# Mask additions of the attention loop tied behind the latest sums of products

## Chip, cores and metric

The kernel runs on one core of one Trainium2 chip. The metric is the device time of one execution in microseconds (us). A core has a matmul engine (TensorE, PE in the profile, with its weight loads as PEld), a vector engine (VectorE, DVE), an activation engine (ScalarE, ACT), a general engine (GpSimd, POOL) and an engine that here only orders transfers (SyncE, SP). Each runs its own queue of instructions in order; semaphores join them.

## The reference, cut to what matters

The program is one inference step of a two-layer trunk over 512 prompt tokens and 8 x 16 sample tokens: a gMLP layer, then a layer of forgetting attention (FoX) with 16 heads of 128. The change touches the attention alone:

```python
def fox_attend_prompt(q, k, v, logf):      # 512 queries, in blocks of 128
    cT = jnp.cumsum(logf, axis=1).transpose(0, 2, 1)
    ...
        s = jnp.einsum('bqhd,bkhd->bhqk', qi, k).astype(jnp.float32) * scale
        s = s + ci[..., :, None] - cT[:, :, None, :]
        s = jnp.where(key_pos[None, :] <= qpos[:, None], s, -jnp.inf)
        p = jax.nn.softmax(s, axis=-1).astype(v.dtype)
        return jnp.einsum('bhqk,bkhd->bqhd', p, v)

def fox_attend_sample(q, k_new, v_new, logf_new, k_cache, v_cache, logf_cache):
    # 16 new queries of each sample against 256 cached keys and 16 new ones
    ...
    mask = jnp.arange(P + T)[None, :] <= (P + jnp.arange(T))[:, None]
    s = jnp.where(mask, s, -jnp.inf)
```

The term of the query's own row falls out of the softmax, so the kernel subtracts only a row of cumulated forget logarithms over the keys ("the decay row") from the scores, with 1e30 added where the causal mask forbids a key.

## The kernel before, in words

**Stages.** Up to about 570 us the first layer runs. The attention loop follows, to about 1140 us, and then the second layer's output projection, gate and stores. In the loop, step `p` (0 to 6) does two things at once. TensorE computes four projections, `project_z(p)` for the pair of heads 2p and 2p+1 and `project_v`, `project_k`, `project_q` for the next pair. Between their matmuls stand the *pieces* of the attention of heads 2p and 2p+1. The last pair's attention (p = 7) runs beside `project_z(7)` and the output projection.

**Projections.** Each of the four is written with seven block products instead of eight (`seven_products`). Each product is 12 matmuls (helper `mm3`, lines 271 to 273) into one of four banks (`UZ`), and DVE adds it to the partial sums: lines 573, 575, 578, and line 562 in `total`, four times in a projection (behind its fourth, fifth, sixth and seventh product). That frees the bank. `total` also notes its instruction as the latest one on DVE:

```python
        def total(i, j, a, b):
            behind["dve"] = nc.vector.tensor_tensor(out=into(i, j), in0=a, in1=b, op=ALU.add)
            done(i, j, into(i, j))
```

`project_z` follows each of its totals with a tanh on ACT (line 957) and a product on DVE (line 958). The weights come by transfers from GpSimd's queue, are combined on GpSimd (line 210), and are split into a high and a low part by ACT (lines 288, 291) and DVE (lines 289, 292).

**Prompt pieces.** For each head and each block i of 128 queries, `scores(i)` prepares the masked decay row of the diagonal block (line 993, into one of two small tiles that take turns: `w1s`, shown as R, and `blk`, shown as CST), multiplies the scores on PE, and takes the row maximum while subtracting the decay row: line 1003 for the blocks left of the diagonal, line 1006 for the diagonal block with line 993's tile. ACT exponentiates (line 1010), DVE inverts and scales (lines 1014, 1015), PE transposes (line 1021) and multiplies with the values (line 1028). The decay row of a head is one transfer from `c_sc`, broadcast to 128 partitions (tiles `sff` and CST).

**Sample pieces.** For each pair of heads and each group of four samples (`bg` 0 and 1), `scores` adds the 16-column causal mask to the last columns of `Wc` (line 1074), multiplies on PE (line 1077), takes the row maximum with `Wc` (line 1080), exponentiates on ACT (line 1083), and lets ACT order the next 128x272 mask rows from `cs_sc` into the same `Wc` (`load_mask`). `Wc` exists once. Lines 1089, 1097, 1105, 1112 and 1118 are the rest of this softmax, its transposes and its products. The cached keys come in by 128 KB transfers on SyncE's queue (`load_k`, four for each block, into one tile) and are turned by DVE in `turn_k` (line 1054, four transposes).

**Order.** `interleave` runs a projection and starts each piece when the sum of the planned matmul times passes the piece's time. In a loop step the four projections end at 12.35, 24.7, 37.0 and 49.4 of that time; the two sample scores have the times 5 and 26, the prompt scores 4, 8.8, 13.6, 18.4 for the first head and 23.2, 28, 32.8, 37.6 for the second. That fixes the order in which instructions are traced. The order in each engine's queue is not the traced one: a planner with its own estimates of durations fills the queues (`schedule_with_timeline_sim=True`), and puts an instruction where its inputs are ready by its estimate. A block under `queued("dve")` gives the planner one more rule: each DVE instruction traced in it stands in DVE's queue behind the instruction noted as `behind["dve"]`. It is an order in one queue, with no semaphore. `turn_k` has it already:

```python
        with queued("dve"):
            for bl in range(4):
                nc.vector.transpose(out=kt[:, hh, bl, :PAST], in_=kraw[:, bl])
```

Of the kernel before, what the change touches and what calls it, by code (L numbers as in the profile page):

```python
# [20 lines left out]
ALU = mybir.AluOpType  # L21
# [10 lines left out]
TS = 16  # L32
PAST = 256
# [7 lines left out]
C_ID, C_BLK, C_CM, C_SEL, C_TRI, C_T16, C_M16, C_N = 0, 128, 256, 384, 640, 1152, 1168, 1184  # L41
# [16 lines left out]
def hybrid_trunk(tc, x_prompt, x_sample, ck, cv, clf, p_prompt, p_sample, norm_pre, norm_post,  # L58
                 g_win, ln_g, ln_b, w_s, b_s, g_wout, f_win, b_f, f_wout, w_proj, w_gate, consts,
                 y_p, y_s, st_v, fk_p, fv_p, fl_p, fk_s, fv_s, fl_s):  # L60
    nc = tc.nc
# [12 lines left out]
    CST = sbuf.tile([P, C_N], F32, name="CST")  # L74
# [15 lines left out]
    def r1(o, n, p=P):  # L90
        return R1[:p, o:o + n]
# [6 lines left out]
    def ring(name, lst):  # L98
        i = counters.get(name, 0)
        counters[name] = i + 1  # L100
        return lst[i % len(lst)]

    def bank(lst=(0, 1, 2, 3, 4, 5, 6, 7)):
        return PB[ring(("bank", lst), lst)]
# [21 lines left out]
    @contextmanager  # L126
    def queued(*engines):

        with ExitStack() as stack:
            for e in engines:  # L130
                stack.enter_context(tc.issue_after(behind[e].ins))
            yield
# [145 lines left out]
    causal = CST[:, C_CM:C_CM + P]  # L278
# [184 lines left out]
    for p in range(4):  # L463
# [3 lines left out]
        out = [bank((0, 1, 2, 3, 4, 5, 6, 7)) for _ in range(NT)]  # L467
# [390 lines left out]
    def v_of(p):  # L858
        return r1(o_v + (p % 2) * 1280, 1280).rearrange("p (t n) -> p t n", t=NT)
# [4 lines left out]
    def q_of(h):  # L864
        return both(o_q, h % 2)[:, :512]

    def k_of(h):
        return both(o_k, h % 2)[:, :512]
# [4 lines left out]
    def z_of(h):  # L873
        return both(o_z, h % 2)
# [93 lines left out]
    def w0_of(h):  # L968
        return tri if h % 2 else SF[:, 2048:2560] if h < 14 else r1(o_raw, 512)

    def load_w0(h, queue=None):
        dma(w0_of(h), c_sc[h].partition_broadcast(P), queue)

    def prompt_pieces(h):

        p, hh = h // 2, h % 2
        q, k, v = q_of(h), k_of(h), v_of(p)
        w0 = w0_of(h)
        zs = (NW - 1) * 2048
        qh, ql, kh, kl = (W[:, zs + z * 512:zs + (z + 1) * 512] for z in range(4))  # L980
        O = PB[7]
        prs, pts = {}, {}

        def setup():
            split(kh, kl, k)
            split(qh, ql, q)

        def scores(i):
            n = (i + 1) * P
            d = slice(i * P, n)  # L990
            S = bank(ATT)
            w1 = ring("w1", w1s)
            nc.vector.tensor_tensor(out=w1, in0=w0[:, d], in1=causal, op=ALU.add)
            if i:
                mm3(S[:, :n], (qh[:, d], ql[:, d]), (kh[:, :n], kl[:, :n]), True, True)
            else:
                nc.tensor.matmul(S[:, :n], q[:, d], k[:, :n], start=True, stop=True)
            pr = prs[i] = r1(o_P + ring("P", (0, 1)) * 512, 512)
            m = small()
            init = -3e38  # L1000
            if i:
                m0 = small()
                nc.vector.tensor_tensor_reduce(out=pr[:, :i * P], in0=S[:, :i * P], in1=w0[:, :i * P], scale=1.0, scalar=init,
                                               op0=ALU.subtract, op1=ALU.max, accum_out=m0)
                init = m0
            nc.vector.tensor_tensor_reduce(out=pr[:, d], in0=S[:, d], in1=w1, scale=1.0, scalar=init,
                                           op0=ALU.subtract, op1=ALU.max, accum_out=m)
            nm, sm = small(), small()
            nc.vector.tensor_scalar(out=nm, in0=m, scalar1=-1.0, scalar2=None, op0=ALU.mult)  # L1009
            nc.scalar.activation(out=pr[:, :n], in_=pr[:, :n], func=AF.Exp, bias=nm, accum_out=sm)  # L1010
            if i == 3 and h + 2 < 14:
                load_w0(h + 2, nc.scalar)
            ri = small()
            nc.vector.reciprocal(out=ri, in_=sm)
            nc.vector.tensor_scalar(out=pr[:, :n], in0=pr[:, :n], scalar1=ri, scalar2=None, op0=ALU.mult)  # L1015

        def turn(i):
            n, pr = (i + 1) * P, prs[i]
            tb = bank(ATT)
            for j in range(i + 1):  # L1020
                nc.tensor.transpose(out=tb[:, j * P:(j + 1) * P], in_=pr[:, j * P:(j + 1) * P], identity=ident)
            pt = pts[i] = r1(o_PT + ring("PT", (0, 1)) * 512, 512)
            nc.scalar.activation(out=pt[:, :n], in_=tb[:, :n], func=AF.Copy)

        def values(i):
            d, pt = slice(i * P, (i + 1) * P), pts[i]
            for j in range(i + 1):
                nc.tensor.matmul(O[:, d], v[:, j, hh * P:(hh + 1) * P], pt[:, j * P:(j + 1) * P], start=(j == 0), stop=(j == i))  # L1028
            if i == 3:
                nc.vector.scalar_tensor_tensor(out=y_of(h)[:, :512], in0=O, scalar=0.5, in1=z_of(h)[:, :512], op0=ALU.mult, op1=ALU.mult)  # L1030

        return setup, scores, turn, values
# [27 lines left out]
    Wc = r1(o_Ws, 272)  # L1060
# [4 lines left out]
    def sample_pieces(p, bg):  # L1065

        pr = r1(o_Ps, 400)
        pt = r1(o_PTs, 384)
        os_ = r1(o_Ps, 256)
        kept = {}  # L1070

        def scores():
            S = bank(ATT)
            nc.vector.tensor_tensor(out=Wc[:, PAST:], in0=Wc[:, PAST:], in1=CST[:, C_M16:C_M16 + TS], op=ALU.add)
            for hh in range(2):
                for bl in range(4):
                    nc.tensor.matmul(S[32 * bl:32 * bl + 32, :272], qpads[:, hh, 4 * bg + bl].rearrange("p h q -> p (h q)"),
                                     kt[:, hh, bl], start=(hh == 0), stop=(hh == 1))
            m, nm, sm, ri = small(), small(), small(), small()
            nc.vector.tensor_tensor_reduce(out=pr[:, :272], in0=S[:, :272], in1=Wc, scale=1.0, scalar=-3e38, op0=ALU.subtract,  # L1080
                                           op1=ALU.max, accum_out=m)
            nc.vector.tensor_scalar(out=nm, in0=m, scalar1=-1.0, scalar2=None, op0=ALU.mult)
            nc.scalar.activation(out=pr[:, :272], in_=pr[:, :272], func=AF.Exp, bias=nm, accum_out=sm)
            if 2 * p + bg < 15:
                load_mask(2 * p + bg + 1, nc.scalar)
            nc.vector.reciprocal(out=ri, in_=sm)
            kept["ri"] = ri

            nc.vector.tensor_tensor(
                out=pr[:, 272:].rearrange("p (b k) -> p b k", b=NB),  # L1090
                in0=CST[:, C_SEL + bg * P:C_SEL + (bg + 1) * P].rearrange("p (b k) -> p b k", b=NB),
                in1=pr[:, PAST:272].unsqueeze(1).broadcast_to([P, NB, TS]), op=ALU.mult)

        def turn():
            tb = bank(ATT)
            for j, o_ in enumerate((0, P, 272)):
                nc.tensor.transpose(out=tb[:, j * P:(j + 1) * P], in_=pr[:, o_:o_ + P], identity=ident)
            nc.scalar.activation(out=pt, in_=tb[:, :384], func=AF.Copy)

        def values():  # L1100
            O = bank(ATT)
            nc.tensor.matmul(O[:, :256], pt[:, 256:], v_of(p)[:, 4], start=True, stop=False)
            for t in range(2):
                for bl in range(4):
                    nc.tensor.matmul(O[32 * bl:32 * bl + 32, :256], pt[:, t * P + 32 * bl:t * P + 32 * bl + 32],
                                     vv[:, bl, t], start=False, stop=(t == 1))
            nc.scalar.activation(out=os_, in_=O[:, :256], func=AF.Copy, scale=kept["ri"])

        def gate():
            tb = bank(ATT)  # L1110
            for hh in range(2):
                nc.tensor.transpose(out=tb[:, hh * P:(hh + 1) * P], in_=os_[:, hh * P:(hh + 1) * P], identity=ident)
            for hh in range(2):
                h = 2 * p + hh
                cs = slice(512 + 64 * bg, 512 + 64 * bg + 64)
                y = y_of(h)[:, cs].rearrange("p (b q) -> p b q", b=4)
                o_ = tb[:, hh * P:(hh + 1) * P].rearrange("p (b h q) -> p b h q", b=4, h=2)[:, :, hh, :]
                nc.vector.scalar_tensor_tensor(out=y, in0=o_, scalar=0.5, in1=z_of(h)[:, cs].rearrange("p (b q) -> p b q", b=4),
                                               op0=ALU.mult, op1=ALU.mult)

        return scores, turn, values, gate

    def prompt_times(h, t0, step):
# [107 lines left out]
```

## Time and profile before

| what | before |
|---|---|
| median of 3 runs | 1348.92 us (1347.77 to 1350.22) |
| profiled execution | 1350.09 us, its span 1348.2 us |
| mean granted TensorE clock | 0.990 |
| PE busy in 600 to 1140 us | 499.35 of 540.00 us |
| DVE busy in 600 to 1140 us | 428.70 of 540.00 us |
| executions of line 993 | 64, median 0.28 us each |
| executions of line 1074 | 16, median 0.18 us each |

How to read it: the span runs from the first to the last instruction of the profiled execution. Busy time is the time in which an engine executes; what an engine waited for is inferred from the semaphores. In rows of a timeline the columns are start, duration, engine, line, operation, output and inputs, and in brackets the idle time of the engine just before and what ended it. A group's row has the count, the busy time, the mean in ns, and the idle time before. In rows of a stretch: its bounds and length, then the busy time of PE, weight loads, DVE, ACT and POOL, the granted clock, the DMA share and GB/s. A `q` behind an engine's name is its sequencer, which orders transfers.

### The profile page before, as it was taken

How to read it: one execution, taken by the hardware profiler on the slowest of the kernel's cores; microseconds unless marked ns; L12 is line 12 of the kernel's file. 1: busy time of each engine (PE TensorE's matmuls, PEld its weight loads, DVE VectorE, ACT ScalarE, POOL GpSimd, SP SyncE). 2: the span in 40 equal slices, each digit the busy share in tenths (PEclk: the TensorE clock that was granted, in tenths of full speed). 3: DMA queues.
4: the chain of work that ended last, by engine and by line, in shares of the span. 5: the costliest groups of instructions: out<-in, count | busy, mean ns of one | idle time of the engine just before them, and what ended most of it. 6: DMA issues, size and time to landing. Idle time of an engine off the chain costs nothing.

```text
span 1348.2 us, 21163 instructions
## 1 busy us (share of the span) xinstructions
PE 1294.5 (96%) x7873; PEld 1148.6 (85%) x7873; DVE 971.9 (72%) x1888; ACT 583.4 (43%) x1062; POOL 357.1 (26%) x322
## 2 busy tenths in 40 slices
PE   8999999999999999989989899998889999999998
PEld 6888999999888888877878889887878988788887
DVE  7744999998734646978676878798777987754543
ACT  5433555444543334543343444444434444545431
POOL 1012445442000101353333424454243531000100
PEclk9999999999999999999989999999989999999999
DMA  6432343322433115467776758676676757832211
GB/s 221 141 94 71 118 130 105 100 79 95 129 110 125 63 41 145 125 121 123 163 135 141 159 142 179 153 160 120 123 136 143 178 133 204 296 128 73 78 56 55
DMA packets 275545, 171.53 MB, mean 127 GB/s; under 512 B 188721, under 2 KB 238689, under 8 KB 275442
## 3 DMA queue, kind: packets, MB, share of 16 engines
q1 hardware_dynamic: 261770, 128.63, 34.9%
q0 software_dynamic: 9760, 36.05, 13.5%
q10 hardware_dynamic: 3912, 5.50, 1.2%
q8 instruction: 62, 1.02, 0.3%
q14 instruction: 41, 0.34, 0.1%
HBM read 148.55 MB, written 21.59 MB: 126 GB/s over the span
## 4 chain that ended last, share of the span: by engine, by line
PE 67%; DVE 16%; DMA 10%; issue 4%; ACT 1%; SPq 1%; POOL 0%; DVEq 0%; ACTq 0%; POOLq 0%
PE pb L271 20%; PE pb L273 19%; PE pb L272 19%; DMA R<-cs_sc 6%; DVE W L289 3%; DMA R<-in_cache_fox_k 3%; DVE R L1054 2%; DVE W L292 2%; DVE R L562 2%; PE pb L1028 1%; PE pb L315 1%; SPq L124 1%; PE pb L594 1%; DVE R L958 1%; DVE R L1015 1%
## 5 line engine op out<-in xcount | busy, mean ns | idle before, releaser
L271 PE MATMUL pb<-A,W 128*128 128x320 f32 (+1 forms) x752 | 243.4, 324 | 1.5 <-ACT A L288 0.6
L273 PE MATMUL pb<-A,W 128*128 128x320 f32 (+1 forms) x752 | 235.6, 313 | 0.0
L272 PE MATMUL pb<-A,W 128*128 128x320 f32 (+1 forms) x752 | 235.4, 313 | 0.0
L289 DVE TENSOR_TENSOR W<-RAW,W 128x1024 fp32r<-128x1024 f32 (+1 forms) x126 | 162.4, 1290 | 74.6 <-ACT W L288 72.2
L271 PE MATMUL pb<-W,A 128*128 128x512 f32 x520 | 204.8, 394 | 2.2 <-ACT A L288 1.3
L272 PE MATMUL pb<-W,A 128*128 128x512 f32 x520 | 203.6, 392 | 0.3 <-DVE W L289 0.3
L273 PE MATMUL pb<-W,A 128*128 128x512 f32 x520 | 202.7, 393 | 0.6 <-DVE A L289 0.6
L288 ACT ACTIVATE W<-RAW 128x1024 fp32r<-128x1024 f32 (+1 forms) x126 | 119.8, 951 | 96.1 <-PE pb L273 48.3
L271 PEld LDWEIGHTS pb<-A,W 128*128 128x128 f32 x752 | 143.7, 191 | 4.0 <-DVE R L562 1.1
L272 PEld LDWEIGHTS pb<-A,W 128*128 128x128 f32 x752 | 143.6, 191 | 0.8 <-issue 0.4
L273 PEld LDWEIGHTS pb<-A,W 128*128 128x128 f32 x752 | 143.2, 190 | 0.8 <-issue 0.4
L271 PE MATMUL pb<-tbf,W 128*128 128x320 f32 x360 | 118.3, 328 | 5.1 <-DVE R L562 5.1
L210 POOL TENSOR_TENSOR sff<-RAW 128x512 f32<-128x512 f32 x46 | 60.9, 1326 | 220.5 <-DVE W L289 90.5
L301 POOL TENSOR_TENSOR SML<-SML 128x1 f32<-128x1 f32 x25 | 18.5, 741 | 375.3 <-DVE SML L299 370.6
L271 PEld LDWEIGHTS pb<-W,A 128*128 128x128 f32 x520 | 97.9, 188 | 23.0 <-ACT A L288 2.2
L273 PEld LDWEIGHTS pb<-W,A 128*128 128x128 f32 x520 | 97.8, 188 | 20.6 <-DVE A L289 0.9
L272 PEld LDWEIGHTS pb<-W,A 128*128 128x128 f32 x520 | 98.0, 188 | 20.2 <-DVE W L289 0.5
L272 PE MATMUL pb<-tbf,W 128*128 128x320 f32 x360 | 113.1, 314 | 0.0
L273 PE MATMUL pb<-tbf,W 128*128 128x320 f32 x360 | 112.5, 313 | 0.0
L1010 ACT ACTIVATE R<-R,SML 128x128 f32<-128x128 f32 (+1 forms) x64 | 35.9, 560 | 139.7 <-DVE SML L1009 139.6
L562 DVE TENSOR_TENSOR R<-R,pb 128x320 f32<-128x320 f32 x184 | 85.8, 477 | 3.4 <-PE pb L273 1.9
L271 PEld LDWEIGHTS pb<-tbf,W 128*128 128x128 f32 x360 | 68.6, 191 | 14.9 <-issue 6.2
(267 smaller groups left out, 2836.3 us busy)
## 6 DMA issues: line engine op xcount, KB each, us to landing
RAW<-in_fox_w_in POOLq DMA_DIRECT2D x46, 512.0 KB, 7.0
RAW<-in_gmlp_w_in SPq DMA_DIRECT2D x40, 512.0 KB
R<-in_cache_fox_v SPq DMA_DIRECT2D x32, 512.0 KB
R<-in_cache_fox_k SPq DMA_DIRECT2D x128, 128.0 KB
RAW<-in_gmlp_w_out SPq DMA_DIRECT2D x16, 512.0 KB
RAW<-in_ple_w_gate SPq DMA_DIRECT2D x16, 512.0 KB
RAW<-in_fox_w_out SPq DMA_DIRECT2D x16, 512.0 KB
R<-in_fox_w_in POOLq DMA_DIRECT2D x14, 512.0 KB, 8.1
```

The source lines that it names most:

```text
L124: behind["sp"] = nc.sync.dma_start(out=out, in_=in_)
L210: nc.gpsimd.tensor_tensor(out=o, in0=a, in1=b, op=op)
L271: nc.tensor.matmul(out, lh, rh, start=start, stop=False)
L272: nc.tensor.matmul(out, lh, rl, start=False, stop=False)
L273: nc.tensor.matmul(out, ll, rh, start=False, stop=stop)
L288: nc.scalar.activation(out=hi, in_=src, func=AF.Copy)
L289: nc.vector.tensor_tensor(out=lo, in0=src, in1=f(hi), op=ALU.subtract)
L292: nc.vector.scalar_tensor_tensor(out=lo, in0=src, scalar=times, in1=f(hi), op0=ALU.mult, op1=ALU.subtract)
L301: nc.gpsimd.tensor_tensor(out=q, in0=t, in1=mhalf, op=ALU.pow)
L562: behind["dve"] = nc.vector.tensor_tensor(out=into(i, j), in0=a, in1=b, op=ALU.add)
L1010: nc.scalar.activation(out=pr[:, :n], in_=pr[:, :n], func=AF.Exp, bias=nm, accum_out=sm)
L1054: nc.vector.transpose(out=kt[:, hh, bl, :PAST], in_=kraw[:, bl])
```

## The change

The two mask additions, of the prompt scores (64 executions) and of the sample scores (16), are traced under `queued("dve")`. Each is thus tied behind the latest sum of products that was traced before it. Nothing else is edited.

```diff
@@ -990,7 +990,8 @@
             d = slice(i * P, n)
             S = bank(ATT)
             w1 = ring("w1", w1s)
-            nc.vector.tensor_tensor(out=w1, in0=w0[:, d], in1=causal, op=ALU.add)
+            with queued("dve"):
+                nc.vector.tensor_tensor(out=w1, in0=w0[:, d], in1=causal, op=ALU.add)
             if i:
                 mm3(S[:, :n], (qh[:, d], ql[:, d]), (kh[:, :n], kl[:, :n]), True, True)
             else:
@@ -1071,7 +1072,8 @@
 
         def scores():
             S = bank(ATT)
-            nc.vector.tensor_tensor(out=Wc[:, PAST:], in0=Wc[:, PAST:], in1=CST[:, C_M16:C_M16 + TS], op=ALU.add)
+            with queued("dve"):
+                nc.vector.tensor_tensor(out=Wc[:, PAST:], in0=Wc[:, PAST:], in1=CST[:, C_M16:C_M16 + TS], op=ALU.add)
             for hh in range(2):
                 for bl in range(4):
                     nc.tensor.matmul(S[32 * bl:32 * bl + 32, :272], qpads[:, hh, 4 * bg + bl].rearrange("p h q -> p (h q)"),
```

## The prediction

> **What bounds the kernel now.** I read the page first: TensorE (PE) is busy nearly all the time, so only its few idle stretches and its slow stretches can be won. The chain of work by line then names a strange guest: the transfer of the sample mask rows from `cs_sc`, 6% of the span, on a kernel that is bound by matmuls.
>
> ```profile
> PE 1294.5 (96%) x7873; PEld 1148.6 (85%) x7873; DVE 971.9 (72%) x1888; ACT 583.4 (43%) x1062; POOL 357.1 (26%) x322
> ...
> PE pb L271 20%; PE pb L273 19%; PE pb L272 19%; DMA R<-cs_sc 6%; DVE W L289 3%; DMA R<-in_cache_fox_k 3%; DVE R L1054 2%; DVE W L292 2%; DVE R L562 2%; PE pb L1028 1%; PE pb L315 1%; SPq L124 1%; PE pb L594 1%; DVE R L958 1%; DVE R L1015 1%
> ```
>
> Next the busy time of the engines in the attention loop, as one stretch (columns: length, then PE, weight loads, DVE, ACT, POOL busy, granted clock, DMA share, GB/s):
>
> ```profile
> 600.00:1140.00 540.00, 499.35 (x3539) 452.87 (x3539) 428.70 (x1049) 225.28 (x458) 208.79 (x203) 0.97 0.70 149
> ```
>
> PE is idle for 540.00 - 499.35 = 40.65 us here, most of the 54 us (1348.2 - 1294.5) that it is idle in the whole span, and the clock granted is 0.97. Then the waits of the vector engine (DVE) in that stretch:
>
> ```profile
> DVE R L1074 <- DMA R<-cs_sc: 67.2, 13, 8.6
> DVE R L1054 <- DMA R<-in_cache_fox_k: 9.1, 3, 3.3
> ```
>
> In 13 of its 16 executions the addition of the 16-column sample mask (L1074) stands in DVE's queue before its mask rows have landed, and all DVE work behind it stands still, 67.2 us together. The order of DVE's instructions in time shows who wants it:
>
> ```profile
> 792.22 0.43 DVE L1080 CUSTOM_DVE_ANT_0 R<-pb,R 128x272 f32<-128x272 f32 x1
> ...
> 800.26 0.18 DVE L1074 TENSOR_TENSOR R<-R,CST 128x16 f32<-128x16 f32 x1 [5.47 <-DMA R<-cs_sc]
> ...
> 824.10 0.87 DVE L562 TENSOR_TENSOR R<-R,pb 128x320 f32<-128x320 f32 x2
> ...
> 832.02 0.43 DVE L1080 CUSTOM_DVE_ANT_0 R<-pb,R 128x272 f32<-128x272 f32 x1
> ...
> 838.38 0.18 DVE L1074 TENSOR_TENSOR R<-R,CST 128x16 f32<-128x16 f32 x1 [3.05 <-DMA R<-cs_sc]
> ...
> 861.53 0.47 DVE L562 TENSOR_TENSOR R<-R,pb 128x320 f32<-128x320 f32 x1
> ...
> 865.84 0.43 DVE L1080 CUSTOM_DVE_ANT_0 R<-pb,R 128x272 f32<-128x272 f32 x1
> ```
>
> The mask row's only reader is L1080. The addition waits until 800.26 and is first read at 832.02, 32 us later; the next one waits until 838.38 and is read at 865.84. The wait buys nothing.
>
> **The change, part by part.** *The sample mask (L1074).* The latest sum of products traced before it is the last one of `project_q` for the first group of four samples and the last one of `project_v` for the second (piece times 5 and 26 against part ends at 0 and 24.7). In the rows above these are the L562 at 824.10 (its second) and at 861.53. Both stand after the landing that ended the old wait (by 24 and 23 us), and before the reader (7.1 us from 824.97 to 832.02, 3.8 us from 862.00 to 865.84). So the addition loses its wait and still costs 0.18 us. It issues no transfer; the next mask load is issued by ACT behind the exponential and is not moved. The tie is an order in DVE's own queue, no semaphore; behind the addition stand the row maxima and the weight splits, which stand behind that sum of products today already.
>
> What are 67.2 us of a stopped DVE worth to PE? I cut out the stretch around each of eleven waits, from the transfer's issue to PE's last gap behind it, and read length minus PE busy:
>
> ```profile
> 679.00:693.00 14.00, 10.96 (x66) 10.21 (x66) 5.97 (x20) 4.12 (x9) 4.64 (x5) 0.87 0.62 127
> 716.00:743.00 27.00, 24.28 (x176) 22.49 (x175) 18.41 (x49) 10.10 (x21) 7.52 (x9) 1.00 0.69 127
> 757.00:777.00 20.00, 16.87 (x119) 15.01 (x118) 15.76 (x42) 7.44 (x16) 7.69 (x7) 1.00 0.55 113
> 792.00:818.00 26.00, 24.24 (x176) 22.46 (x176) 18.55 (x51) 9.88 (x22) 8.16 (x10) 1.00 0.59 129
> 832.00:850.00 18.00, 15.90 (x113) 14.18 (x112) 14.85 (x36) 6.82 (x15) 7.64 (x6) 1.00 0.49 100
> 866.00:892.00 26.00, 23.58 (x172) 21.79 (x171) 18.04 (x48) 9.62 (x21) 7.78 (x9) 1.00 0.63 123
> 906.00:927.00 21.00, 16.76 (x116) 14.64 (x116) 15.36 (x40) 7.08 (x15) 7.64 (x6) 1.00 0.56 97
> 942.00:970.00 28.00, 24.11 (x175) 22.33 (x174) 18.71 (x50) 9.48 (x21) 8.43 (x10) 1.00 0.59 108
> 985.00:1003.00 18.00, 12.86 (x75) 12.17 (x74) 9.33 (x27) 5.63 (x13) 3.50 (x3) 0.82 0.76 131
> 1025.00:1051.00 26.00, 23.96 (x175) 22.17 (x174) 17.93 (x48) 9.71 (x22) 7.66 (x9) 1.00 0.62 134
> 1065.00:1082.00 17.00, 16.12 (x116) 14.53 (x115) 14.89 (x39) 7.04 (x15) 8.03 (x6) 1.00 0.48 105
> sum 241.00, PE 209.64 PEld 191.99 DVE 167.79 ACT 86.92 POOL 78.69; mean PE 19.06 PEld 17.45 DVE 15.25 ACT 7.90 POOL 7.15
> ```
>
> PE idles 241.00 - 209.64 = 31.36 us there, three quarters of the loop's 40.65. That is the most that the removed wait can give directly. Two deductions.
>
> First, what is late next. Right behind the addition, in the first half of each pair, stand the four transposes of a cached K block (L1054), whose data come by transfers too:
>
> ```profile
> 764.76 0.17 DVE L1074 TENSOR_TENSOR R<-R,CST 128x16 f32<-128x16 f32 x1 [4.07 <-DMA R<-cs_sc]
> 765.66 1.41 DVE L1054 STREAM_TRANSPOSE R<-R 128x256 f32<-128x256 f32 x4
> ...
> 751.65 5.11 SPq L124 DMA_DIRECT2D R<-in_cache_fox_k  x2
> ...
> 997.00 0.17 DVE L1074 TENSOR_TENSOR R<-R,CST 128x16 f32<-128x16 f32 x1 [8.57 <-DMA R<-cs_sc]
> 997.90 1.42 DVE L1054 STREAM_TRANSPOSE R<-R 128x256 f32<-128x256 f32 x4
> ...
> 981.84 5.53 SPq L124 DMA_DIRECT2D R<-in_cache_fox_k  x2
> ```
>
> At these two places SyncE is still ordering pieces of the K block (until 756.8 and 987.4) about when the mask rows are ordered, so K probably lands as late as they do, and DVE would stop at L1054 instead, one or two sums of products later. I count half of these two rows: -(3.13 + 5.14) / 2 = -4.1.
>
> Second, DVE is dense in itself (428.70 of 540.00 busy; without the 67.2 us it has some 44 us left in which it waits for nothing of this). PE's waits in the same part of the loop for the scaled softmax rows need not all go:
>
> ```profile
> PE pb L1021 <- DVE R L1015: 8.7, 9, 1.6
> ```
>
> These waits stay near one size whatever the length of the mask wait before them, so I count half: -4.4. That leaves 31.4 - 4.1 - 4.4 = 22.9 us.
>
> *The clock.* Two stretches behind mask waits ran below full clock:
>
> ```profile
> 995.00:1008.00 13.00, 9.27 (x33) 8.18 (x33) 10.99 (x26) 4.24 (x10) 6.33 (x5) 0.61 0.42 70
> 688.00:699.00 11.00, 9.12 (x41) 8.61 (x42) 10.32 (x30) 3.96 (x10) 5.93 (x6) 0.69 0.31 62
> ```
>
> The clock not granted is 13.00 x 0.39 = 5.1 us and 11.00 x 0.31 = 3.4 us. With PE kept fed the second goes whole; the first I count half, as its gap: 3.4 + 2.5 = +5.9 us (from 0 to 8.5). [...]
>
> *The prompt mask (L993).* 64 additions of 128x128 move later. All but one wait for nothing today:
>
> ```profile
> 598.59 0.29 DVE L993 TENSOR_TENSOR R<-sff,CST 128x128 f32<-128x128 f32 x1 [7.65 <-DMA sff<-c_sc]
> ```
>
> This one is the first of head 0. Its tie (last sum of `project_q(0)`) is met long before, so the wait for the decay row can stay: I count nothing, at best its 7.65 us of DVE time. The others cost what they cost today, unless they land in POOL's way:
>
> ```profile
> 860.61 0.28 DVE L1006 CUSTOM_DVE_ANT_0 R<-pb,R 128x128 f32<-128x128 f32 x1
> 861.99 0.90 DVE L993 TENSOR_TENSOR R<-CST 128x128 f32<-128x128 f32 x1
> ...
> L993 DVE TENSOR_TENSOR R<-CST 128x128 f32<-128x128 f32 x14 | 7.0, 503 | 0.0
> ...
> L993 DVE TENSOR_TENSOR CST<-CST 128x128 f32<-128x128 f32 x14 | 4.0, 285 | 0.0
> ```
>
> Alone one takes 0.28 us, at worst 0.90; the group with mean 503 holds (7.04 - 14 x 0.28) / 0.62 = 5 slow ones. POOL is busy 208.79 of 540.00, or 39%, so a random place makes 22 of 56 slow, 17 more: 17 x 0.62 = 10.5 us of DVE time; if none collides, 3.1 us less than now. On the path only the eight whose row maximum follows at once (odd heads, first block, tied to the sum just ahead of an L1006 such as that at 860.61) are sure: 8 x 0.28 = 2.2. I take 2 us of loss, near the low end, since without the mask waits DVE has room; the ends are -3.1 and 12.7. [...]
>
> **Sum:** 22.9 + 5.9 - 2.0 = 26.8 us. The profiled execution took 1350.1 us (span 1348.2 and 1.9 around it), 1.2 above the median of the three runs, 1348.92. It becomes 1323.3, and the median 1322.
>
> **The rivals.** *The K transfer takes over (slightly faster).* If K lands as late as the mask in every pair, only the stretches behind the second half of a pair gain (716, 792, 866, 942 and 1025: 2.72 + 1.76 + 2.42 + 3.89 + 2.04 = 12.8), less about 1.5 for the half counted of L1021 and 2 for L993, no clock: 9.3 us, 1340. For it: the two places above and 9.1 us of such waits today. Against: at 838.38 and the other first halves K was ordered some us ahead of the mask rows.
>
> *More than I count.* All 40.65 us of idling and 8.5 us of clock go: 1300. Against: DVE stays dense.
>
> *It does nothing.* The gaps belong to DVE's load and not to its stops: 1349. Against: the gaps sit behind the waits in all eleven stretches.
>
> *Slower: the planner's new order.* The ties change the order in which the planner fills DVE's queue. If a weight split goes ahead of a row maximum that it follows today, the softmax of that block is late by one split:
>
> ```profile
> L289 DVE TENSOR_TENSOR W<-sff,W 128x1024 fp32r<-128x1024 f32 x42 | 50.8, 1210 | 6.5 <-ACT W L288 5.9
> ```
>
> With PE losing 31.36 of 67.2 us, or 0.47 per us of late DVE, 56 such steps cost 56 x 1.21 x 0.47 = 31.8 us; with the gain of 26.8 the time is 1354. It decides from about 47 of the 56. Against: in the rows above the tied sums already stand ahead of the readers, so nothing must be reordered but the additions.
>
> **How the numbers follow.** My forecast, with its own range 1309 to 1336 (gains of 13 to 40 us): 0.66. K takes over, 1336 to 1345: 0.15. More: 0.05. Nothing: 0.05. Slower: 0.09. Less than 0.2% (2.7 us) cannot be told from no change. Faster is 0.66 + 0.15 + 0.05 = 0.86, same 0.05, slower 0.09. The range 1308 to 1343 leaves out the faster case, the last two, and a bit of the K case.
>
> **What would show it.** Right: no wait of L1074 for `cs_sc`; L1074 directly behind an L562 and a few us ahead of L1080; PE idle in the loop down from 40.65 to some 18 us; the clock of the loop above 0.98. The K step: L1054's wait for the K transfer grows from 9.1 to some 15 us, at the first halves. The L993 step: more of them at 0.90. I would be wrong if L1054 stops DVE as long as L1074 did, if the same PE gaps stand without any stop of DVE ahead of them, or if the row maxima come later behind weight splits.

## The result, and the profile after

The changed kernel is faster: 1316.59 us (median of 4 runs, 1315.62 to 1318.47) against 1349.57 us for the kernel before in the same comparison, a ratio of 0.9758 with a 95% interval of 0.9740 to 0.9775. The profiled execution took 1318.47 us (span 1316.6), 31.6 us less than the one before. The forecast was 26.8 us less, 1322 us. Two lines are added, so that line 993 is now 994, 1006 is 1007, 1054 is 1055, 1074 is 1076 and 1080 is 1082; 562 stays.

The page's first part, and the attention loop as one stretch, which now ends at about 1108 us:

```profile
PE 1286.0 (98%) x7873; PEld 1147.1 (87%) x7873; DVE 970.5 (74%) x1888; ACT 587.8 (45%) x1062; POOL 349.1 (27%) x322
...
600.00:1108.00 508.00, 491.30 (x3547) 451.71 (x3547) 426.82 (x1048) 229.93 (x458) 201.05 (x203) 0.98 0.74 159
```

The span lost 31.6 us. PE's idle time fell from 53.7 us (1348.2 - 1294.5) to 30.6 (1316.6 - 1286.0), which is 23.1; its busy time fell by 8.5. In the loop it idles 508.00 - 491.30 = 16.70 us, where it idled 40.65. DVE does as much work as before, 426.82 us against 428.70: nothing was saved in work, only in order. DVE's waits in the same stretch:

```profile
DVE R L1055 <- DMA R<-in_cache_fox_k: 15.0, 4, 8.1
DVE R L562 <- PE pb L273: 12.7, 18, 1.9
...
DVE R L562 <- DMA y_sc<-R: 5.5, 2, 3.9
```

The 67.2 us of waiting for `cs_sc` are gone without a remainder. Waits for the cached K grew from 9.1 to 15.0, and DVE now waits for matmuls (L562 for L273: 12.7 us, 0.8 before), so in most of the loop it has become the engine that runs ahead. One mask addition and its reader in the order of time:

```profile
847.00 0.48 DVE L562 TENSOR_TENSOR R<-R,pb 128x320 f32<-128x320 f32 x1
847.40 0.64 DVE L1076 TENSOR_TENSOR R<-R,CST 128x16 f32<-128x16 f32 x1
...
850.21 0.43 DVE L1082 CUSTOM_DVE_ANT_0 R<-pb,R 128x272 f32<-128x272 f32 x1
```

It stands directly behind the total to which it is tied, and 2.2 us ahead of its reader. Three loop steps one after the other, of 69 us each, show PE without a gap; the last of these stretches holds the one place in the later loop where it still stops:

```profile
720.00:789.00 69.00, 69.00 (x509) 64.00 (x508) 61.89 (x149) 32.60 (x66) 30.19 (x30) 1.00 0.72 173
789.00:858.00 69.00, 69.00 (x509) 64.01 (x508) 61.96 (x150) 32.73 (x65) 30.28 (x31) 1.00 0.72 163
858.00:927.00 69.00, 69.00 (x509) 64.01 (x508) 61.96 (x150) 32.72 (x65) 30.25 (x30) 1.00 0.79 159
...
966.00:990.00 24.00, 19.02 (x117) 17.10 (x116) 20.19 (x48) 8.58 (x19) 7.82 (x6) 0.86 0.60 95
```

PE's whole list of waits in the loop, for comparison with the eleven stretches shown before:

```profile
PE pb L271 <- DVE SML L1007: 5.0, 1, 5.0
PE pb L1022 <- DVE R L1016: 4.2, 4, 1.9
PE pb L271 <- DVE R L578: 3.7, 1, 3.7
PE pb L271 <- DVE R L562: 2.5, 1, 2.5
PE pb L1114 <- DVE SML L1007: 1.8, 1, 1.8
PE pb L906 <- DVE SML L1007: 1.5, 2, 1.3
PE pb L1079 <- DVE R L1120: 0.4, 1, 0.4
```

### The profile page after: what moved, and what is told of

Its sections match the earlier page's. It is cut to its first block, busy times and chain, and to the rows that moved or that the text cites. A ratio compares the mean times of both kernels' runs of the same rounds, so it can differ in the third digit from the quotient of the medians.

```text
span 1316.6 us, 21174 instructions
## 1 busy us (share of the span) xinstructions
PE 1286.0 (98%) x7873; PEld 1147.1 (87%) x7873; DVE 970.5 (74%) x1888; ACT 587.8 (45%) x1062; POOL 349.1 (27%) x322
## 3 DMA queue, kind: packets, MB, share of 16 engines
q0 software_dynamic: 9760, 36.05, 13.7%
## 5 line engine op out<-in xcount | busy, mean ns | idle before, releaser
L273 PE MATMUL pb<-A,W 128*128 128x320 f32 (+1 forms) x752 | 236.3, 314 | 0.0
L273 PE MATMUL pb<-W,A 128*128 128x512 f32 x520 | 203.3, 393 | 0.1
L289 DVE TENSOR_TENSOR W<-RAW,W 128x1024 fp32r<-128x1024 f32 (+1 forms) x126 | 144.8, 1150 | 74.2 <-ACT W L288 71.8
L273 PEld LDWEIGHTS pb<-A,W 128*128 128x128 f32 x752 | 143.0, 190 | 0.8 <-issue 0.4
L273 PEld LDWEIGHTS pb<-W,A 128*128 128x128 f32 x520 | 97.9, 188 | 20.6 <-DVE A L289 0.5
L210 POOL TENSOR_TENSOR sff<-RAW 128x512 f32<-128x512 f32 x46 | 60.8, 1322 | 202.8 <-DVE W L289 97.6
L273 PE MATMUL pb<-tbf,W 128*128 128x320 f32 x360 | 112.0, 311 | 0.0
L562 DVE TENSOR_TENSOR R<-R,pb 128x320 f32<-128x320 f32 x184 | 86.6, 479 | 20.1 <-PE pb L273 13.6
L289 DVE TENSOR_TENSOR A<-R,A 128x640 fp32r<-128x640 f32 (+1 forms) x42 | 34.5, 854 | 61.9 <-ACT A L288 61.9
```

The lines of the kernel that those rows point to most:

```text
L210: nc.gpsimd.tensor_tensor(out=o, in0=a, in1=b, op=op)
L273: nc.tensor.matmul(out, ll, rh, start=False, stop=stop)
L289: nc.vector.tensor_tensor(out=lo, in0=src, in1=f(hi), op=ALU.subtract)
```

## The experiments

The theory (A): the time was lost because one addition waited in DVE's in-order queue for a transfer whose data were needed 30 us later; whatever takes that wait away brings the whole gain. The rivals: the new places of the 64 prompt additions bring a good part (B), or the ties help by reordering DVE's queue and the wait is a bystander (C). Each ratio is to the kernel before on the same chip.

**One tie at a time.** First the sample addition alone:

```diff
+            with queued("dve"):
                 nc.vector.tensor_tensor(out=Wc[:, PAST:], in0=Wc[:, PAST:], ...)
```

> Only the sample mask addition is tied; the prompt mask additions stay free as before. Theory A (the whole gain is the mask wait of 67.2 us in DVE's queue that goes): no wait of the addition for the cs_sc transfer, and a time within 4 us of the changed kernel's, 1313 to 1321. Theory B (the new order of the 64 prompt mask additions brings a good part): at least a third of the 33 us is missing, 1328 or more.

Measured: 1314.58 us, ratio 0.9753 (0.9735 to 0.9770). No wait for `cs_sc` is left. Then the prompt additions alone:

```diff
+            with queued("dve"):
                 nc.vector.tensor_tensor(out=w1, in0=w0[:, d], in1=causal, op=ALU.add)
```

> Only the 64 prompt mask additions are tied; the sample mask addition stays free. Theory A: the addition still waits for cs_sc, some 60 to 70 us in all, and the time is 1345 to 1352, or up to 5 us above before if the later prompt additions cost what the prediction charged. Theory B: 1338 or less.

Measured: 1343.35 us, ratio 0.9961 (0.9947 to 0.9976), a gain of some 5 us that neither theory forecast at that size; the waits of 51.4 us lie below the 60 to 70 of theory A, too. DVE's waits in the loop (600 to 1130 us), where the sample addition has line 1075:

```profile
DVE R L1075 <- DMA R<-cs_sc: 51.4, 13, 7.9
```

And DVE's order in time at one of the thirteen places, then a row of the kernel before, whose addition ran at 800.26:

```profile
863.60 0.29 DVE L1004 CUSTOM_DVE_ANT_0 R<-pb,CST 128x128 f32<-128x128 f32 x1 [1.30 <-PE pb L273]
...
865.84 0.18 DVE L1075 TENSOR_TENSOR R<-R,CST 128x16 f32<-128x16 f32 x1 [1.93 <-DMA R<-cs_sc]
...
800.35 0.28 DVE L1003 CUSTOM_DVE_ANT_0 R<-pb,CST 128x128 f32<-128x128 f32 x1
```

The waits are 15.8 us shorter than before. The order shows one reason: a row maximum of the prompt (line 1004) now stands ahead of the waiting addition, where line 1003 stood behind it before (800.35 behind 800.26). By an estimate from the next run but one, which gives 0.49 us for each us of wait, 15.8 us are worth 7.7, so the 5 us need no other source; no run shows that there is none. The sample tie alone gives the whole gain of both, so B falls; the two ties do not add up.

**The addition left out, without any tie.**

```diff
-            nc.vector.tensor_tensor(out=Wc[:, PAST:], in0=Wc[:, PAST:], ...)
```

> The kernel before without the sample mask addition and without any tie (the causal mask among the 16 new sample keys is left out). Theory A: what matters is that nothing of DVE's queue waits for the mask rows early; the row maximum then is their first reader and finds them landed: 1313 to 1322, as with the tie. Rival C (the tie helps by the order that it forces, not by the wait that goes): the time stays near before, 1340 or more.

This kernel leaves out the causal mask among the new sample keys, so its sample scores differ. Measured: 1311.61 us, ratio 0.9735 (0.9720 to 0.9751). The row maximum became the first reader of the mask rows and finds them landed: no wait for `cs_sc` is left. Without a tie the gain is at least as large, so it does not come from the ties themselves.

**The wait put back into the changed kernel.**

```diff
                 load_mask(2 * p + bg + 1, nc.scalar)
+                nc.vector.tensor_copy(out=small(), in_=Wc[:, :1])
```

> The changed kernel with one more DVE instruction: a copy of one column of the mask rows, traced right behind the order of their load and untied, so that it stands about where the sample addition stood before and waits for the same transfer; its result is not used. It costs some 0.15 us itself, 15 times. Theory A: some 60 us of waits for cs_sc come back, and PE loses about half of that: 1340 to 1350. Rival C: 1317 to 1323.

Measured: 1340.79 us, ratio 0.9958 (0.9939 to 0.9976). The copy stands close to the old place of the addition, one row maximum behind it (at 867.21 us, for example, behind line 1004 at 863.34, as the addition did with the prompt tie alone), and has its wait:

```profile
DVE SML L1088 <- DMA R<-cs_sc: 54.5, 13, 7.5
```

Fifteen copies of one column cannot cost 27 us of DVE's work: DVE's busy time is 971.6 us in this kernel and 970.5 in the changed one. They cost it by standing still. C falls here. The runs also give a price: 54.5 us of waiting cost 0.0200 of 1347 us, or 27 us, and 51.4 us (the prompt tie alone against the sample tie alone) 0.0208, or 28 us. That is 0.49 and 0.55 us of time for each us that DVE stands; the kernel before, 67.2 us and a ratio of 0.9758, gives 0.49.

**What is left: the K block of the sixth loop step.** The changed kernel was timed again beside the next three.

> The changed kernel once more, so that the next three can be set against it on one chip: 1314 to 1319 us, with the K transfer's 8 us stop of DVE near 969 us and the decay row's near 598 us as before.

Measured: 1315.18 us, ratio 0.9758 (0.9733 to 0.9782); DVE's stop in front of the K transposes was 7.9 us there. In the changed kernel's DVE order that stop looks like this, with SyncE's and POOL's orders of transfers at the time:

```profile
960.44 0.47 DVE L562 TENSOR_TENSOR R<-R,pb 128x320 f32<-128x320 f32 x1
969.03 1.42 DVE L1055 STREAM_TRANSPOSE R<-R 128x256 f32<-128x256 f32 x4 [8.11 <-DMA R<-in_cache_fox_k]
...
944.63 5.84 SPq L124 DMA_DIRECT2D out<-R  x5
950.57 0.95 SPq L124 DMA_DIRECT2D R<-in_cache_fox_v  x2
951.61 8.31 SPq L124 DMA_DIRECT2D R<-in_cache_fox_k  x4
...
953.59 0.78 POOL L122 DMA_DIRECT2D RAW<-in_fox_w_in  x1
954.36 0.76 POOL L122 DMA_DIRECT2D R<-in_fox_w_in  x1
```

SyncE sends off the stores of K, then 1 MB of the next V, and only then the four K pieces, whose orders are spread over 8.31 us while two 512 KB weight units are ordered by POOL. From 959 to 965 us the queue on which SyncE's transfers run (q1) moved no packet at all, while POOL's queue (q0) moved 0.63 MB:

```profile
q0 software_dynamic: 169, 0.63, 84.2%
```

The columns are packets, MB and the share of the 16 DMA engines. The edit puts V behind the first K block:

```diff
+    def load_v_behind(p, bg):
+        with queued("sp"):
+            load_v(p, bg)
...
-            pieces += [..., (s1 + 13.5, lambda: load_v(p + 1, 0))]
+            pieces += [..., (46.15, lambda: load_v_behind(p + 1, 0))]
```

> The changed kernel, with the loads of the next pair's cached V rows traced later and tied behind the first K block of the next pair in SyncE's queue. Theory K (what is left of the wait in the sixth loop step is a K block whose orders come behind V's 1 MB and then share the 16 engines with two weight units): the 8.1 us stop near 969 us falls below 3 us, PE's gap of 5.0 us there and the half clock behind it go, and the time is 4 to 8 us less than the changed kernel's. Rival (the orders are late for what stands in SyncE's queue ahead of both, the 16 stores of K): stop and time stay within 2 us.

Measured: 1305.33 us, ratio 0.9687 (0.9662 to 0.9712), 9.9 us below the changed kernel beside it. The K pieces now go out within 2.35 us, and in the stretch behind the former stop PE has no gap and full clock (SyncE's queue, then a row of a stretch):

```profile
947.19 2.35 SPq L124 DMA_DIRECT2D R<-in_cache_fox_k  x4
949.64 1.53 SPq L124 DMA_DIRECT2D R<-in_cache_fox_v  x2
...
960.00:985.00 25.00, 25.00 (x183) 21.91 (x182) 21.29 (x59) 12.85 (x27) 7.33 (x6) 1.00 0.78 140
```

The stop ahead of these K transposes is gone. The sixth step as a whole, in the changed kernel timed beside it and then with the V edit:

```profile
927.00:1000.00 73.00, 68.17 (x485) 62.92 (x485) 59.00 (x140) 32.42 (x65) 28.64 (x28) 0.95 0.75 141
...
927.00:1000.00 73.00, 73.00 (x535) 67.87 (x534) 62.54 (x158) 35.23 (x69) 30.27 (x31) 1.00 0.82 157
```

The theory of the K orders holds, with more gain than its 4 to 8 us: 4.83 us of idling and 73.00 x 0.05 = 3.65 us of clock make 8.5 of the 9.9; the other 1.4 were not traced. The edit moves K ahead of V and of the weight units at once, so which of the two held K back was not separated.

**The same edit on the kernel before, without a tie.**

> The kernel before (no tie) with the V loads behind the first K block. If the mask wait and the K wait lie one behind the other, so that the K transfer decides only once the mask wait is gone: little, a ratio of 0.993 to 1.003. If freeing the transfers also lets the mask rows land earlier: the waits for cs_sc fall by a third or more and the ratio is 0.985 or less.

Measured: 1346.52 us, ratio 0.9998 (0.9982 to 1.0014): nothing. The waits for `cs_sc` are 65.0 us:

```profile
DVE R L1078 <- DMA R<-cs_sc: 65.0, 13, 8.7
```

The two waits stand one behind the other. What brings 9.9 us behind the change brings nothing ahead of it.

**With the sample tie alone.**

> The sample mask addition alone tied, and the V loads behind the first K block. If the tie of the prompt mask additions adds nothing once the sample addition is tied: the same ratio to before as with both ties and the V edit, 0.969, within 0.003. If that tie costs the 2 us that the prediction charged: 0.967.

Measured: 1304.78 us, ratio 0.9690 (0.9670 to 0.9710), against 0.9687 with both ties. The tie of the prompt additions neither helps nor costs once the sample addition is tied. These two, with the V edit, are the fastest versions that were run; they cannot be told apart.

**The decay row of the first head.** The other place where DVE stops long is the first prompt addition, 7.9 us until 598.5 in the changed kernel, with a PE gap of 3.7 us behind it.

```diff
-            pieces += prompt_times(2 * p + hh, t0 + 4 * step * hh, step)
+            pieces += prompt_times(2 * p + hh, t0 + 4 * step * hh + (3.2 if p + hh == 0 else 0), step)
```

By this edit the last 128 queries of head 0 are scored only after the second head's queries and keys have replaced its own, so they are computed from those.

> The changed kernel, with the first head's four score pieces traced 3.2 us later, so that the first prompt mask addition is tied behind the first total of its projection (line 562) and no longer stands ahead of it while the decay row is on its way. If the gap of 3.7 us that PE has at 601 us and the half clock behind it hang on that order: 3 to 7 us less than the changed kernel. If the softmax of the first head, late by the same transfer, only moves the gap: within 2 us.

Measured: 1316.52 us, ratio 0.9773 (0.9750 to 0.9796), no gain. The decay row is found landed, but DVE then meets a K block that is on its way (DVE's order, then PE's):

```profile
598.24 0.92 DVE L994 TENSOR_TENSOR CST<-sff,CST 128x128 f32<-128x128 f32 x1
602.78 1.42 DVE L1055 STREAM_TRANSPOSE R<-R 128x256 f32<-128x256 f32 x4 [3.63 <-DMA R<-in_cache_fox_k]
...
603.33 0.62 PE L1079 MATMUL pb<-R 128*32 128x272 f32 x2 [3.25 <-issue]
```

PE's gap only moved by 2 us. With both edits (the same part of head 0 is changed):

> Both of these edits. If both hold, the sum of their gains, 7 to 15 us below the changed kernel; if only one does, that one's gain.

Measured: 1306.12 us, ratio 0.9690 (0.9666 to 0.9715), the V edit's gain alone.

## Why the prediction was right, step by step

**The sample mask (L1074): right.** The wait went whole, the addition stands behind the tied total, and its reader finds it done. One tie, no addition at all, or the wait put back: three runs agree that this one instruction carried the change.

**PE's idling, 22.9 us forecast for the loop, 23.95 found there (40.65 - 16.70; 23.1 over the whole span): right in sum, by deductions that were off in opposite ways.** Half of the 8.7 us of waits of L1021 for L1015 was kept as DVE's own density. In the later loop none is left (the 4.2 us on L1022's row lie before 720 us), so these 4.4 us were too cautious. A wait that keeps its size whatever the stop before it was still due to the stop, because DVE, once late, worked without a pause for 12 to 17 us. The kernel before shows it: behind the additions at 764.76 and 800.26 DVE next idles just ahead of 777.47 and of 817.87, the second in this row:

```profile
817.87 0.17 DVE L1014 RECIPROCAL SML<-SML 128x1 f32<-128x1 f32 x1 [0.68 <-ACT R L1010]
```

Of the two places where K was thought to land as late as the mask, the first (765) went entirely, 1.6 us too cautious, and the second (997) stayed almost entirely: a PE gap of 4.98 us where 5.14 us of idling were read before, half of which had been counted as gain, 2.4 us too hopeful. Another 2.5 us stayed where 3.04 had been booked as gain, a PE gap behind L562 at 687 us: there DVE waits for a store of the gated rows to `y_sc` (5.5 us in the list above). That transfer was not named in the prediction. In the second profiled execution of the changed kernel this gap is 0.4 us, so it is not a fixed cost. In all 6.0 us were too cautious and 4.9 too hopeful; that they nearly cancel is luck.

**What is late next: right in sum, less so in place.** K's waits were forecast to grow from 9.1 to some 15 us, at first halves; they are 15.0, and 18.4 in the second profiled execution, that of the kernel timed again. The growth is one stop of 8.1 us in the sixth step; the other waits lie before 720 us, as before. The rival in which K takes over everywhere did not come: in the other steps of the later loop DVE finds K landed.

**The clock, 5.9 us forecast, 5.1 found: near in sum, but not from the places that were named.** From 570 us to the end of the loop the granted clock is 1.00 in both kernels but for a stretch at 600 us (9 us at 0.62 in both) and the following ones, first in the kernel before and then in the changed one:

```profile
675.00:680.00 5.00, 4.46 (x28) 2.75 (x29) 4.26 (x16) 1.92 (x4) 2.27 (x4) 0.66 0.97 189
688.00:698.00 10.00, 8.12 (x34) 7.61 (x35) 9.33 (x26) 3.10 (x8) 5.93 (x6) 0.66 0.25 58
995.00:1009.00 14.00, 10.27 (x46) 8.78 (x49) 11.96 (x30) 4.28 (x11) 6.33 (x5) 0.63 0.45 72
...
686.00:697.00 11.00, 9.97 (x64) 9.05 (x65) 8.92 (x27) 4.19 (x9) 5.19 (x5) 0.84 0.59 99
971.00:980.00 9.00, 7.09 (x35) 6.10 (x37) 9.00 (x20) 2.76 (x7) 6.52 (x5) 0.62 0.51 77
```

Length times the clock not granted gives, with 3.4 us at 600 in each, 3.4 + 1.7 + 3.4 + 5.2 = 13.7 us before and 3.4 + 1.8 + 3.4 = 8.6 now. The stretch at 688 was to go whole and kept 1.8 us, the one of the sixth step kept 3.4 of 5.2 where half was forecast to stay, and the one at 675, which the prediction does not name, went.

What stands ahead of the slow stretch at 686 now is one PE gap:

```profile
687.03 0.42 PE L271 MATMUL pb<-A,W 128*128 128x320 f32 x1 [2.48 <-DVE R L562]
```

Behind it the clock is 0.50 from 688.5 to 691 us. The 3.04 us of idling in the kernel before (14.00 - 10.96 in the prediction's row from 679 to 693) were mostly one gap too: 2.49 us, until 689.33, and the clock is 0.50 from 689.5 to 696 us there. In both kernels, then, it fell behind a gap of 2.5 us. A gap's length alone does not decide, though: in the kernel before, one of 2.71 us until 953.51 left the clock at 1.00 (the prediction's row from 942 to 970).

**The prompt mask (L993): the cost was forecast on the path, and it isn't there.** Its size as DVE time was even underrated. Its four large groups, after (count, busy us, mean ns):

```profile
L994 DVE TENSOR_TENSOR CST<-sff,CST 128x128 f32<-128x128 f32 x14 | 10.9, 778 | 0.0
L994 DVE TENSOR_TENSOR R<-CST 128x128 f32<-128x128 f32 x14 | 9.1, 652 | 0.0
L994 DVE TENSOR_TENSOR CST<-CST 128x128 f32<-128x128 f32 x14 | 9.0, 640 | 0.0
...
L994 DVE TENSOR_TENSOR R<-sff,CST 128x128 f32<-128x128 f32 x13 | 5.4, 412 | 0.0
```

These 55 additions take 34.4 us where the same four groups took 18.6 (7.0 + 4.0 + 4.0 + 3.6 for 54), 15.8 more, against an upper end of 10.5. Two of the rows before are in the prediction; the other two are

```profile
L993 DVE TENSOR_TENSOR CST<-sff,CST 128x128 f32<-128x128 f32 x13 | 4.0, 304 | 0.0
...
L993 DVE TENSOR_TENSOR R<-sff,CST 128x128 f32<-128x128 f32 x13 | 3.6, 279 | 0.0
```

They meet POOL's weight sums more often than by chance, with a mean of up to 0.78 us: 30 of the 64 take more than 0.35 us, where POOL's 39% would make it 25, and each of the 30 ends some 0.15 us after one of these sums. Before there were 7, which end 0.15 us after such a sum as well; with the sample tie alone there is none. One of them beside such a sum:

```profile
827.56 1.39 DVE L994 TENSOR_TENSOR CST<-sff,CST 128x128 f32<-128x128 f32 x1
...
827.50 1.30 POOL L210 TENSOR_TENSOR sff<-sff,RAW 128x512 f32<-128x512 f32 x1
```

This one took 1.39 us instead of 0.28 and ends 0.15 us after the sum (828.95 and 828.80). As a charge on the path the cost did not come: with the tie and without it the ratios are 0.9758 and 0.9753, and 0.9687 and 0.9690 with the V edit. DVE, busy for 426.82 of the loop's 508.00 us, had the room once it no longer stood still. The 2.0 us of loss were a mis-sized term.

**The sum.** 26.8 us forecast, 31.6 found between the two profiled executions. The difference of 4.8 is the 2.0 of L993, 0.2 of idling (23.1 over the whole span) and 2.6 in PE's busy time: that fell by 8.5 us where the clock alone (5.9) had been forecast to lower it. The clock explains at most 5.1. Where the other 3.4 lie was not settled; busy ends of matmuls are modelled, so short stalls inside busy stretches may be counted there.

**The slower rival** (the planner puts weight splits ahead of row maxima) did not come. DVE's order did change in many places, but three differently ordered kernels without the wait (both ties, one tie, no addition) lie within 0.0023 of each other in ratio.

## What to carry to other kernels

In an in-order queue the cheapest-looking instruction can be the dearest (here one of 0.18 us, with 67.2 us of waits in 13 executions): look for waits on a transfer whose reader comes much later, and ask what stands behind the waiting instruction. A planner with its own estimate of a transfer can put such an instruction too early; tying it behind an instruction that surely comes later had no cost that these runs show. When such a wait goes, look at once for the next transfer that the same engine waits for: here moving the K block forward was worth nothing before (0.9998) and another 9.9 us after.

## What the runs showed of the hardware that was not expected

The granted clock fell to 0.50 soon after a PE gap of 2.48 us (to 687.03 in the changed kernel) and after one of 2.49 us (to 689.33 in the kernel before), but it stayed at 1.00 after one of 2.71 us (to 953.51 in the kernel before). While two 512 KB loads of POOL's queue ran, from 959 to 965 us, SyncE's queue moved no packet, though all four K pieces had been ordered by 959.92. DVE's mask additions of 128x128 took up to 1.39 us beside POOL's sums, five times their 0.28 alone.
